# Splitting the first input projection's weights on VectorE, moving a block of constants, adding idle passes, and a new hand-written order

## The chip, the core and the metric

The kernel runs on one core of one Trainium2 chip. The core has a matrix engine (TensorE, written PE in the profile), three engines for elementwise work (VectorE, DVE; ScalarE, ACT; GpSimd, POOL), a queue that issues transfers (SyncE, SP) and 16 DMA engines behind it. Each engine works through its own instructions in order and waits for semaphores where it needs another's result. The metric is the device time of one execution in microseconds.

## The reference, cut to what matters

One layer over 256 latent tokens of 1024 channels, with 256 context tokens, batch 1, all in float32:

```python
mod_l = silu(c) @ w_ada + b_ada              # shifts, scales, gates
zl = modulate(rms_norm(x, norm1_g), sh1, sc1) @ w_in       # 1024 -> 2048 columns
zc = modulate(rms_norm(ctx, norm1_g), csh1, csc1) @ w_in   # same for the context
conv_l = silu(layer_norm(dwconv31(zl[:, :512] * sigmoid(zl[:, 512:1024]))))
lru_l = (forward_scan + backward_scan of gated coefficients) * gelu(zl[:, 1536:])
x = x + g1 * (concat(conv_l, lru_l) @ w_out)
h2 = modulate(rms_norm(x, norm2_g), sh2, sc2)
x = x + g2 * hier_moe(h2, ...)     # top group of 4, top 2 of its 8 experts
out = rms_norm(x, final_g)         # 32 experts, three 1024 x 1024 matrices each
```

The experts' weights are 32 x 3 x 4 MB = 402 MB; everything ahead of them reads some 40 MB.

## The kernel before

The kernel has two parts. The **prologue** computes everything up to the router's choice and the gather of the tokens of the first four experts. The **expert stage** streams all 32 experts' weights through nine tiles of 2 MB (`wide0` to `wide8`); expert by expert it multiplies, gates, turns, multiplies down and scatters back. In it the matrices w1 and w3 are read by `up` (line 874 issues the loads, line 877 multiplies).

*Memory.* The prologue's large buffers are 17 slots of 1 MB (`slot()`), handed out and taken back as the program goes; a float32 tile of 128 x 2048 fills one. When the prologue's pools are closed, the nine wide tiles take over the same memory, two slots to a tile, the ninth also over the `t512` buffers, among them those that the gather of line 815 reads. A wide tile is loaded as soon as everything that lay below has been used for the last time. `WORDER` is the order in which the nine are taken; all their loads are issued by SP, in that order, behind the prologue's own loads.

*First stage of the prologue.* Products that need more than one pass of precision are made from a high and a low half: `split_hi` copies a weight tile to a rounded format, `split_lo` subtracts that from the original (lines 298 to 303). The first projection (`vgproj`, line 331) goes in four quarters of 256 input channels. For quarter q: load the modulation weights and multiply (`ada_first`, line 244), copy the row out (`ada_rows`, ScalarE), turn it (`ada_turn`, TensorE), add bias and scale into columns (`ada_h`, VectorE, lines 268 and 273), modulate the activations (`modulated`: high half on ScalarE, line 292; rest and low half on VectorE, lines 293 and 294), split the quarter's weights (`load_wz`, `split_hi`, `split_lo`), and multiply for four column tiles. `ZH` and `ZL` name the engine of the high and the low half for each quarter (S ScalarE, V VectorE, G GpSimd). The weights of quarter q+1 are split ahead of its columns. The decay constants of the recurrent part (`kh`, `nkh`, lines 204 to 227) are computed on VectorE, with one exponential on ScalarE, ahead of the first quarter.

*Middle.* From the last quarter of `vgproj` on, all engines' work is issued in an order written out by hand, `ORDER`: each word is a step, the letter its kind, digits its arguments, `*n` a repetition. Each engine takes its own instructions from it in that order. The steps that matter here: `v` vgproj's last quarter for one column tile, `h`/`o` high and low half of the second projection's weights (ScalarE, GpSimd), `l` the gated unit that opens the convolution, `u` the second projection, `t` a convolution tap on VectorE, `s` one whose product is made on ScalarE and added on GpSimd, `i` the same with the product on VectorE (line 484), `b` a step of the later modulation, `I`/`J` high and low half of an output-projection weight (engines in `WH`, `WL`; only the third of four is split), `X` the same for its other operand, `O` a pass of the output projection (line 680), `M C Q R N` the layer norm, `n` the scans, `T` the router's top choices, `P` positions of tokens (line 750), `F` one-hot matrices (line 770), `Z` halves of the normed tokens (lines 781 and 303), `G` the gather's matmuls (line 815), `U` its results, `B` a small turn, `W` n idle passes (`warm(n)`, matmuls of ones into a bank that nobody reads, line 154).

## Time and profile before

| | us |
|---|---|
| median of the runs | 1118.24 |
| lowest, highest of 3 | 1113.62, 1120.35 |
| profiled execution, its time | 1117.2 |
| profiled execution, its span | 1115.4 |
| TensorE busy / weight loads | 1001.6 / 446.5 |
| VectorE, ScalarE, GpSimd busy | 311.7, 173.6, 104.0 |
| DMA, mean over the span | 399 GB/s |

All rows are of one profiled execution. A row of a timeline has start, duration, engine, line, operation, what is written and read, and in brackets the idle time ahead of it and what ended it. "PEclk" is the share of TensorE's full clock that was granted: 1.00 is 2.4 GHz, 0.50 is 1.2 GHz. Work of one engine that another hides costs nothing; what counts is what ended the wait of the next.

### The profile page before, as it was taken

The numbers are of one execution on the slowest core, as the hardware profiler recorded it, in microseconds if no ns is written. First come the engines' busy times: TensorE is split into PE (matmuls) and PEld (weight loads), VectorE is DVE, ScalarE is ACT, GpSimd is POOL, SyncE is SP. The second block draws the span as 40 slices with busy tenths as digits, with TensorE's granted clock in tenths as the row PEclk, the third lists the DMA queues.
The fourth block names the chain that finished last, engine by engine and source line by source line (L and its number), as shares of the span: only waits on it lengthen the run. The fifth ranks groups of instructions, "written<-read, shape, count | busy, mean of one in ns | idle before, by whom it ended". The sixth has DMA issues, their size and how long they took to land.

```text
span 1115.4 us, 11881 instructions
## 1 busy us (share of the span) xinstructions
PE 1001.6 (90%) x4973; PEld 446.5 (40%) x4973; DVE 311.7 (28%) x627; ACT 173.6 (16%) x329; POOL 104.0 (9%) x106
## 2 busy tenths in 40 slices
PE   7889998999999998988898898899898989898796
PEld 6764546343434342333333333233333333232244
DVE  4788975221121112111211121112121111111132
ACT  3457943200001000000000000000000000000002
POOL 2487443000000000000000000000000000000001
PEclk9899998999999999999999999999999999999998
DMA  9766759999999999999999999999999999999995
GB/s 360 273 228 266 300 201 420 386 431 431 431 430 430 430 431 431 432 430 429 430 430 432 431 432 430 430 429 431 429 432 431 430 430 431 431 432 431 430 415 198
DMA packets 48480, 445.21 MB, mean 399 GB/s; under 512 B 4084, under 2 KB 14372, under 8 KB 22053
## 3 DMA queue, kind: packets, MB, share of 16 engines
q1 hardware_dynamic: 48210, 443.84, 94.7%
q8 instruction: 41, 0.67, 0.2%
q10 hardware_dynamic: 210, 0.55, 0.1%
q14 instruction: 19, 0.15, 0.0%
HBM read 443.32 MB, written 1.05 MB: 398 GB/s over the span
## 4 chain that ended last, share of the span: by engine, by line
DMA 54%; PE 30%; DVE 1%; POOL 0%; issue 0%; ACT 0%; SPq 0%; DVEq 0%; POOLq 0%; ACTq 0%
DMA wide<-in_w_dram 54%; PE bank L877 20%; PE bank L789 3%; PE bank L680 2%; PE bank L898 2%; PE bank L815 1%; PE bank L1004 1%; PE bank L1134 0%; PE bank L511 0%; PE bank L537 0%; PE bank L1163 0%; PE bank L721 0%; PE bank L1043 0%; POOL xg L1179 0%; PE bank L891 0%
## 5 line engine op out<-in xcount | busy, mean ns | idle before, releaser
L877 PE MATMUL bank<-wide,xg 128*64 128x512 f32 x1984 | 449.0, 598 | 74.6 <-DMA wide<-in_w_dram 74.6
L877 PEld LDWEIGHTS bank<-wide,xg 128*64 128x64 f32 x1984 | 141.8, 137 | 366.1 <-issue 257.0
L877 PE MATMUL bank<-wide,gt 128*64 128x512 f32 x992 | 219.9, 595 | 1.3 <-DVE gt L1006 1.0
L987 DVE TENSOR_TENSOR sl<-sl,bank 128x512 f32<-128x512 f32 x31 | 21.3, 687 | 463.7 <-issue 440.1
L877 PEld LDWEIGHTS bank<-wide,gt 128*64 128x64 f32 x992 | 68.4, 137 | 140.4 <-issue 137.9
L1023 DVE TENSOR_TENSOR yy<-bank,g2bc 64x512 f32<-64x512 f32 x62 | 42.7, 689 | 191.9 <-PE bank L877 191.4
L1179 POOL TENSOR_TENSOR xg<-x,fgbc 128x256 f32<-128x256 f32 x6 | 4.7, 806 | 907.9 <-DVE x L1173 907.9
L980 ACT ACTIVATE sl<-bank 128x512 f32<-128x512 f32 x31 | 18.5, 597 | 431.0 <-PE bank L877 431.0
L789 PE MATMUL bank<-oh,xn 128*128 128x256 f32 x224 | 61.1, 416 | 0.0
L789 PEld LDWEIGHTS bank<-oh,xn 128*128 128x128 f32 x224 | 54.4, 327 | 11.4 <-issue 11.4
L898 PE MATMUL bank<-yy,st 128*128 128x512 f32 x120 | 58.0, 606 | 0.0
L1007 ACT COPY gt<-bank 128x256 f32<-128x256 f32 x31 | 11.5, 372 | 221.0 <-DVE gt L1006 221.0
L903 DVE TENSOR_TENSOR x<-x,bank 128x512 f32<-128x512 f32 x60 | 39.7, 683 | 7.1 <-PE bank L898 7.1
L795 ACT ACTIVATE xg<-bank,gsp 128x256 f32<-128x256 f32 x32 | 17.8, 563 | 153.5 <-PE bank L789 149.0
L303 POOL TENSOR_TENSOR slot<-slot 128x2048 fp32r<-128x2048 f32 x7 | 32.3, 4626 | 35.7 <-ACT slot L298 26.2
L331 PE MATMUL bank<-slot 128*128 128x256 f32 x192 | 28.4, 307 | 7.5 <-ACT slot L292 6.3
L898 PEld LDWEIGHTS bank<-yy,st 128*128 128x128 f32 x120 | 20.6, 191 | 26.5 <-issue 23.2
L798 DVE TENSOR_SCALAR xg<-bank,gsp 128x256 f32<-128x256 f32 x32 | 17.2, 543 | 47.2 <-ACT xg L795 47.1
L331 PEld LDWEIGHTS bank<-slot 128*128 128x128 f32 x192 | 26.2, 209 | 9.6 <-ACT slot L292 7.2
L377 PE MATMUL bank<-slot 128*128 128x512 f32 x96 | 22.9, 394 | 1.5 <-POOL slot L303 1.5
L1004 PEld LDWEIGHTS bank<-ident,sl 128*128 128x128 f32 x124 | 19.5, 204 | 11.1 <-issue 7.1
L487 POOL TENSOR_TENSOR xn<-xn,fgbc 128x256 f32<-128x256 f32 x30 | 22.5, 750 | 2.3
(255 smaller groups left out, 691.8 us busy)
## 6 DMA issues: line engine op xcount, KB each, us to landing
wide<-in_w_dram SPq DMA_DIRECT2D x186, 2048.0 KB, 38.7
slot<-in_wada_dram SPq DMA_DIRECT2D x16, 1024.0 KB, 7.0
slot<-in_wada_dram SPq DMA_DIRECT2D x16, 512.0 KB, 8.9
slot<-in_win_dram SPq DMA_DIRECT2D x8, 1024.0 KB, 7.9
wide<-in_w_dram SPq DMA_DIRECT2D x8, 1024.0 KB, 29.2
slot<-in_wout_dram SPq DMA_DIRECT2D x4, 1024.0 KB, 9.0
wide<-in_w_dram SPq DMA_DIRECT2D x8, 512.0 KB, 11.8
x<-in_x_dram SPq DMA_DIRECT2D x2, 512.0 KB, 4.2
```

The lines of the kernel that those rows point to most:

```text
L303: en.tensor_tensor(lo, w, f(hi), OP.subtract)
L331: P.matmul(pvg[ct][:, i * T:(i + 1) * T], wz[k // 2][wi][:, k % 2, c:c + 128], x[k // 4][:, k % 4, 0:T], start=k + i + n == 0, stop=k == 7 ...
L377: P.matmul(pu, w, x[k // 4][:, k % 4], start=k + n == 0, stop=k == 7 and n == 2)
L487: G.tensor_tensor(acc, acc, p, OP.add)
L680: P.matmul(p, m[:, q], w[:, c:c + 512], start=first and n == 0, stop=len(done) == 8 and n == len(passes) - 1)
L789: P.matmul(pg[:, i * 256:(i + 1) * 256], xn[:, t, quad(k)], oh[:, t].rearrange("p e s -> p (e s)"), start=t + i == 0, stop=t == 1 and i == ...
L877: P.matmul(ps[64 * h:64 * h + 64, :], xs(k4 * 4 + i), w[:, i, h * 512:(h + 1) * 512], start=k4 + i == 0, stop=k4 * 4 + i == 7, tile_positi ...
L898: P.matmul(pz, st[:, t * 128:(t + 1) * 128], yy[:, h * 512:(h + 1) * 512], start=True, stop=True)
L903: V.tensor_tensor(x1[:, t, q], x1[:, t, q], pz, OP.add)
L987: V.tensor_tensor(gg, sl, pb, OP.mult)
L1004: P.transpose(pt[:, j * 128:(j + 1) * 128], gg[:, quad(j)], ident)
L1023: V.tensor_tensor(yy[o:o + 64, h * 512:(h + 1) * 512], py[64 * h:64 * h + 64, :], g2bc[64 * h:64 * h + 64, h * 512:(h + 1) * 512], OP.mult)
```

## The change

- `ZL`: the low halves of the first projection's weights go from GpSimd to VectorE; in each quarter the columns and activations (`prepare`) now come ahead of the split of the quarter's weights, and a second computation of the first columns is gone.
- The decay constants move from ahead of the first quarter to the second pass of the loop, behind the split of quarter 2.
- `WH`: the high half of the split output-projection weight goes from VectorE to ScalarE. (`WL` changes only in a place that is not used.)
- `W4` and `W5`, four and five idle passes, stand ahead of `P0` and `F0`.
- `ORDER` is otherwise rearranged: nine `i` and 44 `s` in place of seven and 46, `l2` and one `b` earlier, scans `n31` and `n21` and several `O` and `G` in other places. `WORDER` is new.

```diff
--- before.py
+++ after.py
@@ -22,7 +22,7 @@
 SLOTS = 17
 WIDE = 9
 
-WORDER = (0, 7, 5, 2, 1, 6, 4, 3, 8)
+WORDER = (2, 7, 0, 6, 1, 3, 5, 4, 8)
 
 
 SP = 384
@@ -31,15 +31,15 @@
 
 
 ORDER = """
-v0 h0 o0 l0 v2 t v3 t h1 v1 t o1 u0 t*4 l2 u1 l1 t b t s b s t*2 s*2 t s t*2 s*2 t i t*2 s t l3 s*2 i t s t*4 s b t*2
-s t c1 t*2 s*3 t s*2 t*2 s*2 t s i t c0 b*2 s u2 s*2 t p10 c2 s t s t p11 t s p00 b s a10 t a00 t i*2 u3 w b t*2 p20 t
-i t*2 p01 s*2 c3 t p30 s*2 t*2 s t d10 s*2 i p21 t a20 s*2 t*2 d00 t a30 t d30 s t b t b z0 t s t a01 r1 d20 s q10 s*2
-t*2 b t*2 s L0 t*2 s q20 t*4 L4 z1 I0 s q30 t p31 q00 t n00 t*2 n20 s b d01 a11 M b a31 k1 C2 z2 C1 a21 n10 C0 L2 d11
-C3 d21 q11 b q21 q01 d31 z3 Q n01 b R e0 N1 N2 X1 N0 I2 L6 x b X2 N3 X0 n30 J2 J0 O001 e3 q31 O112 I4 e2 X3 n11 I6
-O012 O111 O010 J4 b e1 O002 O100 O011 O110 g O113 n31 O102 n21 m1 X5 j J6 m3 O101 O000 O003 X7 O103 m0 O005 O017 O007
-O013 r2 m2 X6 k2 X4 O006 O105 O104 O004 O015 O114 O014 D00 O107 O016 O115 D01 H00 O106 Y0 D10 O117 O116 H01 H10 y D11
-K00 H11 K01 K10 Z0 T0 K11 P0 F0 G06 B G04 G02 Y1 T1 G07 G05 P1 Z1 G03 G00 F1 A1 G01 G10 G11 G12 U0 G16 G17 G14 G15 U4
-U1 G13 U2 U3 U6 U5 U7 A0
+v0 h0 o0 l0 v2 t v3 t h1 v1 t l2 o1 u0 t*4 u1 l1 t b t s b t s t*2 s*2 t s t s*2 t i t*2 s b t s l3 s*2 t s t*4 s b
+t*2 s t c1 t*2 s*3 t s*2 t s*2 t s i t c0 b s u2 s*2 t p10 c2 s t s t p11 t s p00 b i a10 t a00 t i*2 t u3 w b t*2 p20
+t i t*2 p01 s*2 c3 t p30 s*2 t*2 s t d10 s*2 i p21 t a20 s*2 t*2 d00 t a30 t d30 i t b t b z0 t s t a01 r1 d20 i s q10
+s t*2 b t*2 s L0 t*2 q20 t s t*3 L4 z1 I0 s q30 t p31 q00 t n00 t*2 n20 s b d01 a11 M b a31 k1 C2 z2 C1 a21 n10 C0 L2
+d11 C3 d21 q11 b q21 q01 d31 z3 Q n01 b R e0 N1 X1 N2 N0 I2 L6 x b X2 N3 X0 n30 J2 J0 O001 e3 q31 O112 O102 n21 I4 e2
+X3 n11 n31 I6 O012 O111 O010 J4 b e1 O002 O100 O011 O110 g O113 m1 X5 j J6 m3 O101 O000 O003 X7 O103 m0 O017 O007 O013
+r2 m2 X6 k2 X4 O004 O005 O006 O105 O104 O015 O114 O014 D00 O107 O016 O115 D01 H00 O106 Y0 D10 O116 O117 H01 H10 y D11
+K00 H11 K01 K10 Z0 T0 K11 W4 P0 W5 F0 G06 B G04 G02 Y1 T1 G05 P1 Z1 G03 G00 F1 G07 A1 G01 G10 G11 G12 U0 G16 G17 U6
+G14 G15 U4 U1 G13 U2 U3 U5 U7 A0
 """
 VTAPS = (31, 0, 9, 31)
 
@@ -49,11 +49,11 @@
 SQ = ("SGGG", "SSSS")
 LNSQ = "SGSG"
 XC = ("VS", "SV")
-WH, WL = "SSVV", "VVGV"
+WH, WL = "SSSS", "GVGV"
 MH, ML = "GGGGGSSG", "GVGVGVGG"
 GL = ("GG", "GG")
 OS = "0010"
-ZH, ZL = "SSSS", "GGGG"
+ZH, ZL = "SSSS", "VVVV"
 FN = "VS"
 
 
@@ -201,32 +201,6 @@
     first_norm(1, xc)
 
 
-    kh = const.tile([128, 8], F32, name="kh")
-    nkh = const.tile([128, 8], F32, name="nkh")
-    lw = const.tile([128, 5, 8], F32, name="lw")
-    lam = col("lam")
-    V.tensor_scalar(lw[:, 0], lam, -1.0, None, OP.mult)
-    V.tensor_tensor(lw[:, 0], lam, lw[:, 0], OP.max)
-    S.activation(lw[:, 1], lw[:, 0], AF.Exp, scale=-1.0)
-    V.tensor_scalar(lw[:, 2], lw[:, 1], 2.0, None, OP.add)
-    V.reciprocal(lw[:, 2], lw[:, 2])
-    V.tensor_tensor(lw[:, 2], lw[:, 1], lw[:, 2], OP.mult)
-    V.tensor_tensor(lw[:, 3], lw[:, 2], lw[:, 2], OP.mult)
-    V.memset(lw[:, 4], 1.0 / 17.0)
-    for n in (15, 13, 11, 9, 7, 5, 3, 1):
-        V.tensor_tensor(lw[:, 4], lw[:, 4], lw[:, 3], OP.mult)
-        V.tensor_scalar(lw[:, 4], lw[:, 4], 1.0 / n, None, OP.add)
-    V.scalar_tensor_tensor(lw[:, 4], lw[:, 4], 2.0, lw[:, 2], OP.mult, OP.mult)
-    V.tensor_scalar(lw[:, 0], lam, -1.0, 0.0, OP.mult, OP.max)
-    V.tensor_tensor(kh, lw[:, 0], lw[:, 4], OP.add)
-    V.tensor_scalar(kh, kh, 4.0, None, OP.mult)
-    V.tensor_scalar(nkh, kh, -1.0, None, OP.mult)
-    hb = sp[:, COLS["ba"][0]:COLS["bx"][1]]
-    V.tensor_scalar(hb, hb, 0.5, None, OP.mult)
-    dwh = col("dw")
-    V.tensor_scalar(dwh, dwh, 0.5, None, OP.mult)
-
-
 
     mod_a = const.tile([128, 2, 2, 8], F32, name="mod_a")
     g1s = const.tile([128, 2, 8], F32, name="g1s")
@@ -318,7 +292,6 @@
 
     pa = ada_first(0)
     pt = ada_turn(ada_rows(pa))
-    ada_h(0, pt)
     warm(6)
     pvg = [bank() for _ in range(4)]
 
@@ -339,19 +312,45 @@
 
     engines = {"V": V, "S": S, "G": G}
     w = load_wz(0)
+    prepare(0)
     split_hi(*w, engines[ZH[0]])
     split_lo(*w, engines[ZL[0]])
-    prepare(0)
     for q in range(4):
         ks = range(2 * q, 2 * q + 2)
         if q < 3:
             w = load_wz(q + 1)
             rows = ada_rows(ada_first(q + 1))
-            split_hi(*w, engines[ZH[q + 1]])
-            split_lo(*w, engines[ZL[q + 1]])
             vgproj(0, ks)
             pt = ada_turn(rows)
             prepare(q + 1)
+            split_hi(*w, engines[ZH[q + 1]])
+            split_lo(*w, engines[ZL[q + 1]])
+            if q == 1:
+
+                kh = const.tile([128, 8], F32, name="kh")
+                nkh = const.tile([128, 8], F32, name="nkh")
+                lw = const.tile([128, 5, 8], F32, name="lw")
+                lam = col("lam")
+                V.tensor_scalar(lw[:, 0], lam, -1.0, None, OP.mult)
+                V.tensor_tensor(lw[:, 0], lam, lw[:, 0], OP.max)
+                S.activation(lw[:, 1], lw[:, 0], AF.Exp, scale=-1.0)
+                V.tensor_scalar(lw[:, 2], lw[:, 1], 2.0, None, OP.add)
+                V.reciprocal(lw[:, 2], lw[:, 2])
+                V.tensor_tensor(lw[:, 2], lw[:, 1], lw[:, 2], OP.mult)
+                V.tensor_tensor(lw[:, 3], lw[:, 2], lw[:, 2], OP.mult)
+                V.memset(lw[:, 4], 1.0 / 17.0)
+                for n in (15, 13, 11, 9, 7, 5, 3, 1):
+                    V.tensor_tensor(lw[:, 4], lw[:, 4], lw[:, 3], OP.mult)
+                    V.tensor_scalar(lw[:, 4], lw[:, 4], 1.0 / n, None, OP.add)
+                V.scalar_tensor_tensor(lw[:, 4], lw[:, 4], 2.0, lw[:, 2], OP.mult, OP.mult)
+                V.tensor_scalar(lw[:, 0], lam, -1.0, 0.0, OP.mult, OP.max)
+                V.tensor_tensor(kh, lw[:, 0], lw[:, 4], OP.add)
+                V.tensor_scalar(kh, kh, 4.0, None, OP.mult)
+                V.tensor_scalar(nkh, kh, -1.0, None, OP.mult)
+                hb = sp[:, COLS["ba"][0]:COLS["bx"][1]]
+                V.tensor_scalar(hb, hb, 0.5, None, OP.mult)
+                dwh = col("dw")
+                V.tensor_scalar(dwh, dwh, 0.5, None, OP.mult)
             for ct in range(1, 4):
                 vgproj(ct, ks)
     wu = []
```

## Rows read from the trace of the kernel before

**Rows 1.** Windows: stretch, length, busy (x) of PE PEld DVE ACT POOL, PEclk, DMA share, GB/s

```profile
71.00:103.00 32.00, 31.77 (x174) 19.50 (x178) 25.73 (x45) 21.09 (x40) 26.69 (x36) 1.00 0.51 187
...
103.00:138.00 35.00, 31.68 (x175) 15.87 (x168) 32.64 (x58) 32.12 (x55) 17.65 (x22) 1.00 0.88 342
...
29.10:39.30 10.20, 7.28 (x34) 6.70 (x35) 8.05 (x23) 4.03 (x6) 4.29 (x1) 0.54 0.64 237
...
186.00:196.40 10.40, 8.84 (x66) 8.53 (x66) 6.08 (x29) 5.05 (x10) 3.02 (x3) 0.55 1.01 431
...
196.00:200.00 4.00, 4.00 (x19) 2.35 (x21) 1.72 (x6) 1.67 (x4) 0.00 (x0) 1.00 0.49 150
...
200.00:400.00 200.00, 196.80 (x877) 77.23 (x875) 37.70 (x79) 17.14 (x36) 0.00 (x0) 1.00 1.01 430
...
400.00:600.00 200.00, 178.91 (x778) 67.98 (x776) 35.73 (x69) 11.22 (x24) 0.00 (x0) 1.00 1.01 431
```

**Rows 2.** Timeline of SP: the first and the fourth load of wide tiles.

```profile
155.13 1.10 SPq L874 DMA_DIRECT2D wide<-in_w_dram  x2
...
167.40 0.33 SPq L874 DMA_DIRECT2D wide<-in_w_dram  x1
```

**Rows 3.** Waits of SP: who waited for whom, us in total, times, longest.

```profile
SPq L874 <- PE bank L815: 19.0, 1, 19.0
...
SPq L874 <- PE bank L680: 5.2, 1, 5.2
```

**Rows 4.** Timeline of the first stage, quarters 0 to 2.

```profile
20.74 0.17 DVE L211 TENSOR_SCALAR lw<-lw 128x8 f32<-128x8 f32 x1 [5.79 <-ACT lw L210]
...
22.25 0.33 PE L263 MATMUL bank<-ident,t 128*128 128x128 f32 x1 [0.39 <-ACT t L258]
...
22.41 1.50 PE L154 MATMUL bank<-ones 128*128 128x128 f32 x12
...
24.07 4.53 POOL L303 TENSOR_TENSOR slot<-slot 128x2048 fp32r<-128x2048 f32 x1 [9.92 <-ACT slot L298]
...
24.25 4.38 DVE L218 TENSOR_SCALAR lw<-lw 128x8 f32<-128x8 f32 x1
...
30.91 2.08 ACT L292 ACTIVATE slot<-slot,mod_a,g1s 128x256 fp32r<-128x256 f32 x4 [6.92 <-DVE g1s L273]
...
31.56 0.79 PE L331 MATMUL bank<-slot 128*128 128x256 f32 x2 [4.58 <-ACT slot L292]
...
44.75 4.55 PE L331 MATMUL bank<-slot 128*128 128x256 f32 x36
```

**Rows 5.** Timeline, quarter 3 and the start of the middle.

```profile
53.63 4.46 DVE L273 SCALAR_TENSOR_TENSOR g1s<-mod_a,sp 128x2 f32<-128x2 f32 x2
...
62.20 0.39 ACT L441 ACTIVATE t<-bank 128x256 f32<-128x256 f32 x1 [0.28 <-PE bank L331]
...
71.23 8.00 PE L377 MATMUL bank<-slot 128*128 128x512 f32 x34 [1.54 <-POOL slot L303]
```

**Rows 6.** Lines by form: count, duration min/median/max (or busy us, mean ns).

```profile
L294 DVE TENSOR_TENSOR slot<-slot x16: 424/426/428, 32.0 to 61.5; 128x256 fp32r<-128x256 f32 x16
...
L987 DVE TENSOR_TENSOR sl<-sl,bank 128x512 f32<-128x512 f32 x31 | 21.3, 687 | 463.7 <-issue 440.1
...
L298 ACT CAST slot<-slot x6: 1885/1903/1906, 22.1 to 62.5; 128x2048 fp32r<-128x2048 f32 x6
...
L484 DVE TENSOR_SCALAR fgbc<-cb,sp x3: 342/348/348, 97.8 to 109.1; 128x256 f32<-128x256 f32 x3
```

**Rows 7.** Timeline of the routing and the gather.

```profile
186.72 0.61 PE L750 MATMUL bank<-msk,tri 128*128 128x32 f32 x2 [2.75 <-DVE msk L745]
...
188.17 0.81 PE L815 MATMUL bank<-oh,t 128*128 128x256 f32 x2 [0.83 <-DVE oh L770]
...
191.73 2.70 POOL L303 TENSOR_TENSOR t<-xn,t 128x512 fp32r<-128x512 f32 x2 [5.41 <-ACT t L781]
...
192.25 5.39 PE L815 MATMUL bank<-oh,t 128*128 128x256 f32 x22
```

## What is expected of the change

> **What bounds the kernel now.** I read the kernel from its end backwards, with the windows by stretch first. From 200 to 400 and from 400 to 600 us the DMA engines' share is 1.01 at 430 and 431 GB/s, while TensorE gets down to 178.91 busy of 200 us [rows 1]: the expert stage ends when its weights have landed. So I asked when that stream starts to run without a hole. Nine expert loads go into the nine wide tiles before any tile is reused; the first is issued at 155.13 us [rows 2]. The ninth waited 19.0 us for the matmuls of line 815 [rows 3], the gather for the first four experts, because its tile lies over buffers that the gather reads. The last of these matmuls ends at 192.25 + 5.39 = 197.64 [rows 7]. The eight loads ahead of it were through just before: from 196 to 200 the DMA share is 0.49 [rows 1], a hole worth 4 x 0.51 = 2.0 us, the only one from there on. **A microsecond off the end of the gather is therefore a microsecond off the kernel**, as long as eight loads are in by then; a stream that only starts earlier gives nothing, since it waits longer for the ninth tile.
>
> The gather's end hangs on the work in front of it. In 71 to 103 us TensorE is busy 31.77 of 32 us, in 103 to 138 VectorE 32.64 of 35 and ScalarE 32.12 [rows 1]; a shift at 71 us travels through, less what is added on VectorE behind 103. The stage ahead of 62 us (quarter after quarter: modulation columns, activations, weight halves, products) is where the change works. There the columns are late: the turned modulation is ready at 22.25 + 0.33 = 22.58, yet the activations begin at 30.91 [rows 4]. A VectorE instruction on 8 columns takes 4.38 us, from 24.25, exactly under GpSimd's 4.53 us subtraction of the low half; the rest of the constants, and then the columns, stand behind it in VectorE's queue. In the last quarter two column instructions take 4.46 us in the same way [rows 5].
>
> **The change, part by part.**
>
> *Low halves on VectorE (ZL), and columns ahead of them.* The operation is not in the trace on VectorE at 128x2048. By its rows at 256 and 512 elements (0.426 and 0.687 us, 1.02 ns per element) it is 0.687 + 1536 x 0.00102 = 2.25 us [rows 6]; bounds are 2.1 (the slope alone) and 4.6 (GpSimd's own time). I take 2.25. Quarter 0: columns from 22.6 to about 23.1 (one of two computations of them is removed), activations on ScalarE 2.08 us to 25.2, high half 1.90 to 27.1, low half to 29.4. TensorE's products of column tile 0 then wait for 29.4, and their last four (0.126 us each, 4.55 / 36) end at 29.9; before, the first began at 31.56 [rows 4]. Turn at 30.3, columns 30.7, activations and high half (2.08 + 1.90) at 34.8, low half at 37.1. TensorE: 36 products to 34.8, about 2 us of modulation matmuls to 36.8 (their weights have landed: this queue is unchanged up to there), the next quarter's first products to 38.3, turn at 38.6. Quarter 2 likewise: columns 39.1, high half 43.1, low half 45.4; turn of quarter 3 at 46.9.
>
> *Constants later.* They now stand on VectorE between that low half (45.4) and the columns of quarter 3. They are 30 instructions at a pitch of about 0.2 us (from 20.74 to 24.25 eighteen of them begin [rows 4]), plus the hop to ScalarE for one exponential: 6.4 us, so columns 3 start at 51.8 and not at 46.9. At their old place they held the first columns; what waits behind them now are activations, both halves and products of quarter 3. Bounds: 5 us if they follow each other without a gap, and 8 if the hops show. Columns done 52.25, activations 54.35, high half 56.25, low half 58.5. Before, the columns of quarter 3 ended at 53.63 + 4.46 = 58.1 [rows 5], but both halves were ready by then. So of 6 us of lead, about half goes back.
>
> *TensorE in front of the last quarter.* Its products (now ORDER's v0) start at 56.25 after idling from 51.45, 4.8 us. The trace has this case: idle 4.58 us ahead of 31.56 [rows 4], and a granted clock of 0.54 from 29.1 to 39.3 [rows 1], the 1.2 GHz level for nearly all of it. I take half of such a stretch: v0 ends at about 59.6, the tanh that opens the convolution follows there (before: 62.20 [rows 5]), and all 48 products end at 65.2. The second projection's low halves stay on GpSimd; they end at 58.5 + 2 x 4.53 = 67.6; before, TensorE's wait for them ended at 71.23 [rows 5]. With 48 matmuls of 0.235 us (8.00 / 34) from 65.2 on, TensorE is through at 76.5 in place of 71.23 + 8.00 = 79.2. **Shift at this point: -2.7 us**; -3.5 with no fall of the clock, +0.6 if all 48 products run at the low one.
>
> *The middle.* ORDER has nine of the side taps' products on VectorE in place of seven: 2 x 0.35 = +0.7 us [rows 6], in the part where VectorE is the fullest; ScalarE loses as many. Bounds: 0 (ScalarE was as full) and 2, if each also waits for a GpSimd add to end. WH moves the high half of one output-projection weight to ScalarE, 1.90 us [rows 6] in a queue with idle time around 150, and its low half on GpSimd starts some 3 us later. Behind it wait GpSimd's products for the recurrent columns and so the last output-projection passes; ORDER puts these passes later by about as much. I cost it at nothing; without that cover up to 3 us. The removed column computation is worth 0.4 us and is contained above.
>
> *Idle passes.* W4 stands in a hole: TensorE idles 2.75 us ahead of 186.72 [rows 7]. W4's eight rows and W5's ten take 1.0 and 1.25 us at the rate of 12 in 1.50 [rows 4]. W5 fills a wait of 0.83 us and so costs 0.4. From 186.0 to 196.4 the granted clock is 0.55 [rows 1], and 22 gather matmuls take 5.39 us. At full clock 32 of them need 32 x 0.126 = 4.0 us in place of some 8. But the second token tile's low halves leave GpSimd only at 191.73 + 2.70 = 194.43 [rows 7], and five of its eight blocks need or stand behind the later one: ten matmuls, 1.3 us, end at 195.7. **Gain 1.9 us**, not 4. If the clock falls all the same, W5 costs 10 x 0.25 = 2.5 us in the hole of 0.83: **+1.7**. The Trainium skill (TensorE: Matmul & The Clock Gate, Part 1) holds that the throttled state is the default and that sustained activity releases it. By it these passes, at 2.4 GHz, keep the gain; the trace shows the low level through 10.4 us with TensorE busy 8.84 of them, which is why I do not count on it, and by that row the sum would be 3.6 us higher.
>
> *WORDER.* It picks which wide tile is loaded first. A first load before 155.13 [rows 2] is worth nothing by itself, by the argument above; one up to 2.0 us later is free too, since it closes the hole ahead of the ninth.
>
> *Sum*: -2.7 + 0.7 - 1.9 = -3.9. The profiled execution took 1117.2 us (span 1115.4 and 1.8 around it): 1113.3. It lies 1.0 below the median of 1118.24, so the median forecast is **1114.3 us**. All best ends: -3.5 + 0 - 1.9, and near 2 more if the constants take 5 us: 1111. All worst ends of the same mechanism, 0.6 + 1.9 + 1.7: 1122.
>
> **Rivals.**
> *The clock falls anyway ahead of the gather* (the passes don't do what they are for). For: the row of 10.4 us at 0.55. Against: W4 and W5 are full 128-column passes where there was nothing. -2.0 + 1.7 = -0.3: 1118.
> *The lead is lost in the middle*: three engines over 90% busy in 103 to 138, so ORDER's lead dissolves and only the gather's gain stays: 1116.3. For: ScalarE and VectorE are both full. Against: all three are full of the same work as before, started earlier.
> *More than forecast*: the constants' hops are short and the clock holds at 56: about -8: 1110.
> *Slower: the first expert load waits for the output projection.* WORDER begins with tile 2. In the old layout tile 2 was the fourth, and its load waited for output-projection matmuls of line 680 until 167.40 [rows 2, 3]. All wide loads are in one queue behind it. If the new layout has it alike, the first issue is at 167.4 - 2.0 = 165.4, 10.3 us later than before, of which the hole takes 2.0: +8.3, 1126. It decides once the first issue is later than 157.1. Against: the slots are handed out in another order after the change, so tile 2 need not hold the same weights; the trace cannot say.
>
> **How the numbers follow.** Forecast 0.45 (its own range 1111 to 1117), clock falls 0.22, lead lost 0.13, more 0.12, slower rival 0.08. The range 1107 to 1121 leaves out the slower rival and the far end of the better one. One per cent is 11 us, about what a measurement of this kernel can tell from no change; only several best ends together reach it, or a much later first load: faster 0.06, same 0.90, slower 0.04.
>
> **What would show it.** VectorE's low halves near 2.25 us with no VectorE instruction on few columns over 1 us before 56; columns 0 by 23; the constants between 45 and 52 with columns 3 behind them; the tanh near 59.6; line 815's end near 193.7; clock 1.0 from 184 on; the first wide issue before 157.1 and the DMA with a hole only ahead of the ninth. Wrong would be: the ninth load not waiting for the gather, a DMA hole after 200, or TensorE idle inside the output projection.

## The result, and the profile after the change

The median fell from 1118.13 us to 1111.84 us (20 runs of each): ratio 0.995, interval 0.9941 to 0.9959. The gain is half a per cent and clear of none; it is within the 1% that the forecast called "same", 2.5 us below the predicted 1114.3 and inside its range. The profiled execution took 1111.8 us, its span 1110.0 against 1115.4. Line numbers have moved: gather 814 (815 before), wide loads 873 (874), low halves 277 (303), columns 242 (268), first products 304 (331).

The first stage, in order of time (columns as in [rows 4]; the second fence is TensorE alone):

```profile
22.77 0.17 DVE L242 TENSOR_TENSOR mod_a<-bank,sp 128x8 f32<-128x8 f32 x1 [7.85 <-PE bank L237]
...
27.07 2.29 DVE L277 TENSOR_TENSOR slot<-slot 128x2048 fp32r<-128x2048 f32 x1
...
38.24 0.17 DVE L242 TENSOR_TENSOR mod_a<-bank,sp 128x8 f32<-128x8 f32 x1 [1.34 <-PE bank L237]
...
44.76 0.17 DVE L334 TENSOR_SCALAR lw<-sp 128x8 f32<-128x8 f32 x1
...
50.51 0.17 DVE L242 TENSOR_TENSOR mod_a<-bank,sp 128x8 f32<-128x8 f32 x1
...
56.64 9.46 POOL L277 TENSOR_TENSOR slot<-slot 128x2048 fp32r<-128x2048 f32 x2 [42.24 <-ACT slot L272]
...
58.40 0.39 ACT L440 ACTIVATE t<-bank 128x256 f32<-128x256 f32 x1 [1.83 <-PE bank L304]
```

```profile
54.82 1.51 PE L304 MATMUL bank<-slot 128*128 128x256 f32 x8 [4.33 <-ACT slot L272]
...
64.32 11.07 PE L376 MATMUL bank<-slot 128*128 128x512 f32 x48
...
140.09 0.71 PE L166 MATMUL bank<-ident,r 128*128 128x128 f32 x4 [0.41 <-POOL r L160]
...
142.35 5.42 PE L679 MATMUL bank<-slot,xn 128*128 128x512 f32 x12
```

In this stage no VectorE instruction on few columns is long any more where [rows 4, 5] had 4.4 us ones. The low half takes 2.29 us. The constants run from 44.76 to 50.5 with columns 3 behind them, and TensorE idles 4.33 us ahead of the last quarter. The second projection ends at 64.32 + 11.07 = 75.39.

The gather, then the DMA engines around its end (windows: stretch, length, busy of PE PEld DVE ACT POOL, PEclk, DMA share, GB/s), then SP's first wide load and its longest wait for the gather:

```profile
186.10 6.05 PE L814 MATMUL bank<-oh,t 128*128 128x256 f32 x24
...
186.44 2.69 POOL L277 TENSOR_TENSOR t<-xn,t 128x512 fp32r<-128x512 f32 x2 [5.73 <-ACT t L780]
186.53 1.47 DVE L769 TENSOR_TENSOR oh<-iota,posm 128x256 fp32r<-128x256 f32 x1
```

```profile
189.00:190.00 1.00, 1.00 (x6) 1.00 (x6) 0.90 (x5) 0.57 (x1) 0.14 (x1) 1.00 0.86 352
190.00:191.00 1.00, 1.00 (x6) 1.00 (x6) 0.67 (x3) 0.22 (x1) 0.00 (x0) 1.00 0.16 66
191.00:192.00 1.00, 1.00 (x5) 0.95 (x5) 0.00 (x0) 0.62 (x2) 0.00 (x0) 1.00 0.04 16
192.00:193.00 1.00, 1.00 (x7) 0.35 (x7) 0.21 (x1) 0.76 (x2) 0.00 (x0) 1.00 0.00 0
...
196.00:400.00 204.00, 200.80 (x897) 78.67 (x895) 38.08 (x76) 16.77 (x33) 0.00 (x0) 1.00 1.01 431
```

```profile
144.73 0.33 SPq L873 DMA_DIRECT2D wide<-in_w_dram  x1
```

```profile
SPq L873 <- PE bank L814: 19.1, 1, 19.1
```

The first wide load now goes out at 144.73, ten us earlier than in [rows 2], and yet the ninth again waits 19.1 us for the gather. What the early start shows in the DMA engines is a longer hole: 0.14 + 0.84 + 0.96 + 1.00 = 2.9 us without traffic, against 2.0 before [rows 1]. From 196 us on the stream is full (share 1.01, 431 GB/s).

The end of the gather moved from 197.64 [rows 7] to 192.15, by 5.49 us; the span by 5.4. In two pieces: line 166, the norm ahead of the output projection, moved from 144.17 to 140.09, and the way from it to the gather's end shrank from 53.47 to 52.06 us. The kernel before at that place (timeline, then a window):

```profile
144.17 1.20 PE L166 MATMUL bank<-ident,r 128*128 128x128 f32 x4 [0.41 <-POOL r L160]
...
147.98 4.56 PE L680 MATMUL bank<-slot,xn 128*128 128x512 f32 x10
```

```profile
144.00:150.00 6.00, 5.83 (x35) 3.14 (x36) 5.70 (x10) 4.04 (x8) 0.11 (x1) 0.72 0.01 3
```

The table gathers these points for all traces. They are single executions that come out of their start unevenly (column "turn 0", the first turned modulation, at 20.8 to 24.6 us; const_early's 26.5 is its own doing), so lengths are compared rather than points. "Projection" is the end of the second projection's first 48 matmuls. The ratio stands against runs of the kernel before on the same chip; medians of different rows are of different chips, and rows are better compared by their ratios.

| kernel | turn 0 | columns 3 | projection | line 166 | gather's end | span less gather's end | median | ratio, interval |
|---|---|---|---|---|---|---|---|---|
| before | 22.25 | 53.43 | 79.23 | 144.17 | 197.64 | 917.8 | 1118.13 | |
| after | 22.40 | 50.51 | 75.39 | 140.09 | 192.15 | 917.9 | 1111.84 | 0.995, 0.9941 to 0.9959 |
| stage_alone | 24.56 | 52.66 | 77.56 | 142.49 | 194.44 | 924.7 | 1118.00 | 0.9999, 0.9983 to 1.0014 |
| old_worder | 22.40 | 50.50 | 74.41 | 139.12 | 191.78 | 923.7 | 1118.12 | 1.0015, 1.0004 to 1.0025 |
| no_idle | 22.56 | 50.67 | 75.79 | 140.50 | 192.62 | 918.0 | 1113.42 | 0.9953, 0.9938 to 0.9967 |
| contiguous | 22.56 | 50.65 | 74.41 | 139.14 | 192.02 | 917.8 | 1113.70 | 0.9976, 0.9963 to 0.9988 |
| contiguous_write | 20.75 | 49.32 | 73.08 | 137.78 | 190.68 | 917.7 | 1110.91 | 0.9944, 0.9924 to 0.9963 |
| lows_on_vectore | 22.65 | 50.75 | 74.53 | 139.26 | 191.87 | 917.9 | 1111.38 | 0.9941, 0.9918 to 0.9964 |
| low_on_gpsimd | 22.45 | 56.81 | 83.80 | 148.52 | 202.82 | 917.8 | 1120.47 | 1.0034, 1.002 to 1.0047 |
| const_first | 22.38 | 51.15 | 74.86 | 139.57 | 192.35 | 917.8 | 1111.45 | 0.9941, 0.9919 to 0.9962 |
| const_last | 24.59 | 48.36 | 74.53 | 148.16 | 199.93 | 917.8 | 1117.62 | 0.9998, 0.9983 to 1.0013 |
| const_early | 26.53 | 51.33 | 75.09 | 139.80 | 191.63 | 917.9 | 1111.10 | 0.9947, 0.9935 to 0.9959 |
| const_gap | 22.42 | 46.62 | 70.34 | 135.05 | 187.83 | 917.8 | 1106.47 | 0.9902, 0.988 to 0.9925 |
| gap_and_gather | 20.96 | 45.78 | 69.50 | 134.22 | 185.16 | 918.6 | 1106.78 | 0.99, 0.9883 to 0.9916 |

In eleven of fourteen traces the span ends 917.7 to 918.0 us after the gather: its end sets the kernel's. Two that are far off, stage_alone and old_worder, have the old WORDER behind the new first stage in common; of the third, gap_and_gather, below.

Two stretches take longer in some traces than in others, with the same code, where the granted clock is low. Seven traces have the changed first stage (after to lows_on_vectore); from turn 0 to the projection column they take 51.9 to 53.2 us, after 52.99, the kernel before 56.98. In after the clock is 0.50 from 56 to 62 us, while TensorE multiplies; in old_worder, with 52.01, it is 0.50 from 54 to 60, partly while TensorE waits. And the 24 matmuls of line 720 in front of the routing take 2.77 us at the full clock and some 4 at the low one, in seven traces: old_worder, contiguous, contiguous_write, lows_on_vectore, low_on_gpsimd, const_first and const_gap. There the way from line 166 to the gather's end is some 0.8 us longer (52.67 to 52.78 in old_worder, const_first and const_gap, whose gather is the changed kernel's, against 51.8 to 52.1).

### The profile page after: what moved, and what is told of

It reads as the page before. It is cut to its first block, busy times and chain, and to the rows that moved or that the text cites. A ratio compares the mean times of both kernels' runs of the same rounds, so it can differ in the third digit from the quotient of the medians.

```text
span 1110.0 us, 11919 instructions
## 1 busy us (share of the span) xinstructions
PE 1002.1 (90%) x4991; PEld 447.7 (40%) x4991; DVE 303.6 (27%) x629; ACT 175.2 (16%) x328; POOL 84.5 (8%) x102
## 4 chain that ended last, share of the span: by engine, by line
DMA 55%; PE 36%; DVE 4%; POOL 1%; ACT 1%; issue 1%; SPq 0%; POOLq 0%; DVEq 0%; ACTq 0%
DMA wide<-in_w_dram 55%; PE bank L876 20%; PE bank L788 3%; PE bank L679 2%; PE bank L376 2%; PE bank L897 2%; PE bank L304 1%; DVE bank L468 1%; PE bank L510 1%; PE bank L814 1%; PE bank L1003 1%; DVE slot L277 1%; ACT slot L272 0%; PE bank L186 0%; PE bank L396 0%
## 5 line engine op out<-in xcount | busy, mean ns | idle before, releaser
L897 PEld LDWEIGHTS bank<-yy,st 128*128 128x128 f32 x120 | 20.6, 191 | 26.5 <-issue 23.2
L679 PE MATMUL bank<-slot,xn 128*128 128x512 f32 x48 | 22.2, 601 | 0.0
```

The source lines that it names most:

```text
L679: P.matmul(p, m[:, q], w[:, c:c + 512], start=first and n == 0, stop=len(done) == 8 and n == len(passes) - 1)
L897: P.matmul(pz, st[:, t * 128:(t + 1) * 128], yy[:, h * 512:(h + 1) * 512], start=True, stop=True)
```

## Experiments: which part brought the time

**stage_alone.** The first stage as changed, everything behind it as before:

```diff
-WORDER = (2, 7, 0, 6, 1, 3, 5, 4, 8)
+WORDER = (0, 7, 5, 2, 1, 6, 4, 3, 8)
...
-v0 h0 o0 l0 v2 t v3 t h1 v1 t l2 o1 u0 t*4 u1 l1 t b t s b t s t*2 s*2 t s t s*2 t i t*2 s b t s l3 s*2 t s t*4 s b
+v0 h0 o0 l0 v2 t v3 t h1 v1 t o1 u0 t*4 l2 u1 l1 t b t s b s t*2 s*2 t s t*2 s*2 t i t*2 s t l3 s*2 i t s t*4 s b t*2
...
-WH, WL = "SSSS", "GVGV"
+WH, WL = "SSVV", "VVGV"
```

> The changed kernel's first stage (low halves on VectorE, columns ahead of them, constants in the second pass) with ORDER, WORDER and WH of the kernel before, so without idle passes. If the gain was made in the first stage alone: the row of the norm (line 166) starts at 139.4 to 140.1 us as in the changed kernel (140.09; before 144.17), and the kernel takes 1111 to 1112 us unless the clock falls behind it as it did before, which costs 1.5 us. If the new order is what carries the lead through the middle: that row starts at 142 us or later and the kernel takes 1114 to 1118 us.

By its numbers this is the second theory's outcome (line 166 at 142.49, 1118.00 us), but not by its mechanism: line 166 is late only because turn 0 is, at 24.56. From turn 0 to line 166 it takes 117.93 us, the changed kernel 117.69, the one before 121.92; from there to the gather's end 51.95, the changed one 52.06. So the lead of four us is the first stage's. What the new ORDER and WH are worth up to line 166 shows from the projection column on: 64.93 and 64.94 us in stage_alone and before, 64.70 to 64.73 in all traces with the new ORDER but const_last. They save 0.2 us. And yet nothing arrives at the end: 924.7 us from the gather's end on. Waits of SP, then windows:

```profile
SPq L873 <- PE bank L679: 33.7, 3, 21.1
...
SPq L873 <- PE bank L814: 18.5, 1, 18.5
```

```profile
170.00:175.00 5.00, 5.00 (x18) 2.63 (x17) 3.37 (x5) 0.72 (x2) 1.14 (x3) 1.00 0.53 157
190.00:195.00 5.00, 5.00 (x24) 4.58 (x25) 1.97 (x10) 2.51 (x8) 1.25 (x1) 0.92 1.00 424
```

The loads wait for the output projection (line 679), the DMA engines are busy for half of 170 to 175, and at 190 to 195, where the changed kernel has its hole, they are busy throughout: the ninth load waits for the gather as before and goes out behind it, but queues behind others.

**old_worder.** The changed kernel with one line of before:

```diff
-WORDER = (2, 7, 0, 6, 1, 3, 5, 4, 8)
+WORDER = (0, 7, 5, 2, 1, 6, 4, 3, 8)
```

> The changed kernel with the old order of the wide tiles, (0, 7, 5, 2, 1, 6, 4, 3, 8); all else stays. Forecast (an earlier start of the stream is worth nothing, the ninth load waits for the gather): the gather's end stays, the kernel stays at 1111 to 1112.5 us. Theory from the run with the first stage alone (its third load was issued at 172.13 us, behind the output projection, and its gather's end came as early as in the changed kernel, but the kernel was 7 us longer): the third load waits until about 169.7 us, the six behind it need some 29 us, the DMA runs without a hole past the gather's end, and the kernel takes 1117 to 1119.5 us.

The theory taken from stage_alone holds, the forecast's does not: 1118.12 us. The first two loads go out at 155.81 and 156.26, the third at 168.47 behind the output projection. A tile of 128 x 4096 floats is 2.10 MB, by estimate 4.88 us at 430 GB/s; six of them from 168.5 on last to 197.8, past the gather's end at 191.78. SP's issues, from the third load on, then windows:

```profile
168.47 4.05 SPq L873 DMA_DIRECT2D wide<-in_w_dram  x6
```

```profile
165.00:170.00 5.00, 5.00 (x20) 3.15 (x19) 1.96 (x3) 0.58 (x3) 0.00 (x0) 1.00 0.65 226
...
190.00:195.00 5.00, 5.00 (x24) 2.79 (x25) 2.27 (x9) 2.18 (x6) 0.00 (x0) 1.00 1.01 433
```

Without the new WORDER the whole gain is lost (ratio 1.0015 against 0.995). That the new first stage hands out the slots in another order, so that the old tile order no longer fits the times at which tiles come free, is an argument from the program; no run shows which slots lie under which tile, and the new WORDER was not run in the old layout.

**low_on_gpsimd.** The first stage's main edit undone, the rest kept:

```diff
-ZH, ZL = "SSSS", "VVVV"
+ZH, ZL = "SSSS", "GGGG"
```

> The changed kernel with ZL back at GpSimd; columns stay ahead of the weights' halves, all else stays. Forecast's reading (GpSimd needs 4.53 us where VectorE needs 2.29, and VectorE's few-column instructions crawl under it): each of the three quarter steps is 2.2 us longer, the constants take about 10 us because they start under the subtraction of quarter 2, columns 3 come at about 57 in place of 50.5, the second projection's low halves end near 75 in place of 66.1, and the kernel takes 1118 to 1121 us. Rival (the order of columns ahead of the halves is what brought the gain, the engine little): 1112 to 1115 us.

As expected, to the place: columns 3 at 56.81, the second projection's low halves end at 61.15 + 13.63 = 74.78, 1120.47 us. With the columns ahead of the halves, but the low halves on GpSimd, the kernel is slower than the one before. Part of that is the constants, which take 10.1 us here in place of 5.75: in the first row a VectorE instruction on 8 columns lasts exactly as long as GpSimd's subtraction.

```profile
46.88 4.56 DVE L335 TENSOR_TENSOR lw<-sp,lw 128x8 f32<-128x8 f32 x1
...
56.81 0.17 DVE L242 TENSOR_TENSOR mod_a<-bank,sp 128x8 f32<-128x8 f32 x1
```

```profile
46.86 4.56 POOL L277 TENSOR_TENSOR slot<-slot 128x2048 fp32r<-128x2048 f32 x1 [5.30 <-ACT slot L272]
```

## Experiments: the idle passes and the gather

**no_idle.** `W4` and `W5` are taken out of ORDER.

```diff
-K00 H11 K01 K10 Z0 T0 K11 W4 P0 W5 F0 G06 B G04 G02 Y1 T1 G05 P1 Z1 G03 G00 F1 G07 A1 G01 G10 G11 G12 U0 G16 G17 U6
+K00 H11 K01 K10 Z0 T0 K11 P0 F0 G06 B G04 G02 Y1 T1 G05 P1 Z1 G03 G00 F1 G07 A1 G01 G10 G11 G12 U0 G16 G17 U6
```

> The changed kernel without its idle passes W4 and W5; all else stays. Theory of the forecast (the passes keep the clock up, and the clock sets the pace of the gather): the granted clock falls in front of the gather, its last matmul ends about 1.9 us later than 192.15, the kernel takes 1113.7 us against 1111.8. Rival (the gather's matmuls do not follow the clock: 22 in 5.39 us at 0.50 before, 24 in 6.05 us at 1.00 after, 0.245 and 0.252 us each): the clock may fall, but the gather's end moves by -0.4 to +0.3 us and the kernel stays at 1111.4 to 1112.1.

The way from line 166 to the gather's end is 52.12 us without and 52.06 with them. The median, 1113.42, lies near the first theory's 1113.7, but its ratio can't be told from the changed kernel's (0.9953 against 0.995, overlapping intervals), so the traces decide. The clock does what the forecast feared (the gather's last matmuls stand under the windows):

```profile
180.00:185.00 5.00, 2.65 (x39) 2.33 (x40) 3.69 (x21) 0.57 (x2) 0.95 (x4) 0.50 1.03 439
185.00:190.00 5.00, 5.00 (x23) 5.00 (x23) 2.67 (x10) 4.05 (x9) 2.56 (x2) 0.50 1.02 431
```

```profile
186.59 6.02 PE L814 MATMUL bank<-oh,t 128*128 128x256 f32 x24
```

Through these ten us it is 0.50, the 1.2 GHz level; in the changed kernel 0.68 and 0.98: there too it is 0.50 from 182 to 185, in spite of the passes. The gather's last 24 matmuls take 6.02 us here, all at 0.50, and 6.05 there, at 1.00. They do not follow the clock. (The rival's 22 in 5.39 us "at 0.50" were not all at that level: the clock over them is 0.71.) The trace of the kernel before shows it within one stretch of these matmuls:

```profile
193.00:195.00 2.00, 2.00 (x11) 2.00 (x10) 1.12 (x7) 1.15 (x4) 1.43 (x2) 0.50 0.97 418
...
196.00:197.00 1.00, 1.00 (x5) 1.00 (x6) 0.15 (x1) 0.00 (x0) 0.00 (x0) 1.00 0.48 205
```

Eleven in 2 us at 0.50, five in 1 us at 1.00.

**contiguous.** What else sets their pace? A block's 128 weights are picked with a step of four elements, 16 bytes. Here the halves are stored so that they lie side by side:

```diff
-            S.mul(w[1], x1[:, t, q], rstd[:, t:t + 1])
-            split_lo(*w, engines[GL[t][h]])
+            xq, wh, wl = (xn[:, t, q].rearrange("p (c k) -> p k c", k=4),
+                          *(v.rearrange("p (k c) -> p k c", k=4) for v in w[1:]))
+            S.mul(wh, x1[:, t, q].rearrange("p (c k) -> p k c", k=4), rstd[:, t:t + 1])
+            split_lo(xq, wh, wl, engines[GL[t][h]])
...
-            P.matmul(pg[:, i * 256:(i + 1) * 256], xg_s[t, k // 4][n][:, quad(k % 4)],
+            P.matmul(pg[:, i * 256:(i + 1) * 256], xg_s[t, k // 4][n][:, k % 4 * 128:k % 4 * 128 + 128],
```

> The changed kernel with the two halves of the normed tokens for the first gather stored so that a block's 128 channels lie side by side; ScalarE and GpSimd read their inputs with a stride of four elements, TensorE's weights are contiguous. If the stride of the weights sets the pace of the gather (0.24 us a matmul at either clock; the same shape with contiguous weights takes 0.126 us at line 304): line 814's pitch falls to 0.12 to 0.14 us at the full clock, the last low half still leaves GpSimd at about 189.1, the gather ends near 190.9 in place of 192.15, the kernel takes 1110 to 1111 us. Rival (the pace is set by something else, such as the moving side): pitch 0.23 or more, kernel unchanged.

Timeline of TensorE, of ScalarE and of GpSimd, then the weight loads of the changed kernel and of this one (count, duration min/median/max in ns):

```profile
186.67 1.36 PE L816 MATMUL bank<-oh,t 128*128 128x256 f32 x9
189.25 0.96 PE L816 MATMUL bank<-oh,t 128*128 128x256 f32 x6 [1.22 <-POOL t L277]
190.72 1.30 PE L816 MATMUL bank<-oh,t 128*128 128x256 f32 x9 [0.51 <-POOL t L277]
```

```profile
186.40 2.31 ACT L782 ACTIVATE t<-x,rstd 128x512 fp32r<-128x512 f32 x2
```

```profile
187.67 3.00 POOL L277 TENSOR_TENSOR t<-xn,t 128x512 fp32r<-128x512 f32 x2 [6.90 <-ACT t L782]
```

```profile
L814 PEld LDWEIGHTS bank<-oh,t x32: 308/332/336, 182.8 to 191.6; 128*128 128x128 f32 x32
```

```profile
L816 PEld LDWEIGHTS bank<-oh,t x32: 186/188/338, 183.6 to 191.6; 128*128 128x128 f32 x32
```

24 matmuls now take 1.36 + 0.96 + 1.30 = 3.62 us of TensorE in place of 6.05, and a weight load 188 ns in place of 332: the step of the weights sets the pace. (At the low clock, up to 186 us, this kernel's loads take about 330 ns as well and start every 0.22 us, with the step every 0.24: it costs little there.) The gather's end does not come earlier (52.88 us from line 166, where traces with the same low clock in front of the routing have 52.67 to 52.78): ScalarE's two halves take 2.31 in place of 1.33 us, GpSimd's 3.00 in place of 2.69, and TensorE waits 1.22 and 0.51 us for them. The Trainium skill (Advanced Engine Details and Errata, SBUF Cachelines) says that SBUF works in lines of 16 bytes and that each access that goes to another line pays; four floats are such a line, and the trace agrees for TensorE's weights (6.05 against 3.62 us) and for ScalarE's reads (2.31 against 1.33).

**contiguous_write.** The same, but read in order and written with a step, here of 128 elements, 512 bytes (`"p (k c) -> p c k"` on the written side).

> As the run with contiguous gather weights, but with the elements taken in their stored order and written with a stride: ScalarE and GpSimd read in order and write four channels 512 bytes apart. If reading with a stride was what made ScalarE's half 1.15 us in place of 0.66, and writing with one costs nothing: ScalarE 0.66, GpSimd's last low half at 189.1, gather at a pitch of 0.126 us and its end near 190.8, kernel 1110 to 1111 us. Rival (a stride costs the same on either side): ScalarE 1.15 us, gather's end at 192, kernel as the changed one.

ScalarE's halves take 2.15 us, GpSimd's 3.02, the way to the gather's end 52.90: this step on the written side costs about as much. (The runs of contiguous spread from 1110.1 to 1116.5, and its ratio, 0.9976, is worse than this kernel's, 0.9944, and the changed one's; the traces do not explain it.)

**lows_on_vectore.** The other cover by itself: low halves of the second token tile on VectorE.

```diff
-GL = ("GG", "GG")
+GL = ("GG", "VV")
...
-K00 H11 K01 K10 Z0 T0 K11 W4 P0 W5 F0 G06 B G04 G02 Y1 T1 G05 P1 Z1 G03 G00 F1 G07 A1 G01 G10 G11 G12 U0 G16 G17 U6
+K00 H11 K01 K10 Z0 T0 K11 W4 P0 W5 F0 G06 B G04 G02 Y1 T1 G05 P1 F1 Z1 G03 G00 G07 A1 G01 G10 G11 G12 U0 G16 G17 U6
```

> The changed kernel with the second token tile's low halves for the gather on VectorE in place of GpSimd, and F1 ahead of Z1 in ORDER. If GpSimd's lock is what makes the one-hot matrix take 1.47 us (186.53; 0.43 for the first token tile): it takes 0.43, the low halves are done near 188.4 in place of 189.1, and the gather, then held by TensorE's pitch of 0.235 us alone, ends near 191.7 in place of 192.15: kernel 0.3 to 0.5 us shorter, not to be told from none. Rival (VectorE's low halves push the routing behind them, and the gather's results come later): gather's end at 192.5 or later.

The one-hot matrix takes 0.43 us in place of 1.47, the low halves are done at 187.57 + 0.69 = 188.3. The gather's end is 52.61 us behind line 166, at most 0.2 nearer than in traces with the same low clock in front of the routing (52.67 to 52.78): with this cover gone it is held by TensorE's pace.

```profile
186.38 0.43 DVE L769 TENSOR_TENSOR oh<-iota,posm 128x256 fp32r<-128x256 f32 x1
...
187.57 0.69 DVE L277 TENSOR_TENSOR t<-xn,t 128x512 fp32r<-128x512 f32 x1 [0.17 <-PE bank L814]
```

## Experiments: the place of the constants

**const_first.** The block of constants goes back ahead of the first quarter (the reverse of its move in the diff of the change).

> The changed kernel with the decay constants back ahead of the first quarter. Forecast's reading (the constants hold up whatever columns stand behind them, by some 4 to 5 us wherever they are): they run from 20.7 to 26.6, columns 0 come at about 26.8 in place of 22.8, and as the quarters follow one another every 7.7 us, columns 3 come at about 50.0 (now 50.5): the kernel takes 1111 to 1112 us. Rival (only GpSimd's subtraction made them slow at that place): columns 0 by 24, columns 3 by 47.2, kernel near 1108.5.

They end at 26.0 and columns 0 come at 25.98, columns 3 at 51.15: 0.6 us later than in the changed kernel, not 0.5 earlier, since the products of quarter 0 ran at a low clock behind TensorE's wait (36 in 5.71 us in place of 4.56, the clock 0.80 in 34 to 40 us). The last quarter keeps the full clock in return. Line 166 and the median are those of the changed kernel. Moving the block was worth nothing by itself.

**const_last.** The same block behind the loop over the quarters.

> The changed kernel with the decay constants behind the last quarter's low half on VectorE. If they cost what the forecast says at their new place (columns 3 wait for them from 45.9 to 50.5), and a lead at 60 us travels through: columns 3 at 45.9, TensorE's last quarter at about 50.2 with no fall of the clock, the kernel 3 to 4.6 us shorter, 1107.2 to 1108.8. Rival: the taps of the convolution now start behind them on VectorE, the fullest engine of the middle, or the second projection's weights come no sooner, and the lead dissolves: 1111 to 1113 us.

Wrong in its price. The rival had the place, VectorE in front of the taps, but not what makes it dear. Columns 3 do come without a wait and TensorE starts the second projection earlier, but (VectorE, then GpSimd):

```profile
57.41 4.57 DVE L344 TENSOR_SCALAR lw<-lw 128x8 f32<-128x8 f32 x1
62.01 4.48 DVE L343 TENSOR_TENSOR lw<-lw 128x8 f32<-128x8 f32 x1
...
69.35 0.42 DVE L439 SCALAR_TENSOR_TENSOR g2bc<-t,bank 128x256 f32<-128x256 f32 x1
```

```profile
57.37 9.10 POOL L277 TENSOR_TENSOR slot<-slot 128x2048 fp32r<-128x2048 f32 x2 [40.83 <-DVE lw L343]
```

The block meets the second projection's low halves on GpSimd, and two of its instructions take 4.57 and 4.48 us. The convolution opens at 69.35 (its input was ready at 57.57), line 166 comes 123.57 us behind turn 0 (117.69 in the changed kernel), and the gain is gone.

**const_early.** The block in VectorE's idle 7.85 us ahead of the first columns:

```diff
+    V.tensor_scalar(lw[:, 0], lam, -1.0, None, OP.mult)
+    V.tensor_tensor(lw[:, 0], lam, lw[:, 0], OP.max)
+    S.activation(lw[:, 1], lw[:, 0], AF.Exp, scale=-1.0)
     first_norm(1, xc)
+    V.tensor_scalar(lw[:, 2], lw[:, 1], 2.0, None, OP.add)
...
```

> The changed kernel with the decay constants where VectorE idled 7.85 us ahead of the first columns (14.9 to 22.8): their first two instructions and the exponential ahead of the context's norm, the rest behind it. If a lead at the last quarter travels through (in the run with the constants first, 0.5 us at columns 3 gave 0.5 us at line 166): columns 0 stay at 22.8, columns 3 come at 45.9 in place of 50.5, no VectorE instruction on few columns over 1 us, TensorE idles under 1 us ahead of the last quarter, the row of line 166 comes 3 to 4.6 us earlier, the kernel takes 1107.2 to 1109 us. Rival (the middle is bound by VectorE and takes the lead back): under 1 us of gain, 1111 to 1112 us.

Columns 0 come at 26.90, four us late. ScalarE's queue tells why:

```profile
15.22 0.21 ACT L207 ACTIVATE lw<-lw 128x8 f32<-128x8 f32 x1 [8.11 <-DVE lw L206]
15.33 1.04 ACT L178 ACTIVATE xn<-slot 128x1024 f32<-128x1024 f32 x1
```

The exponential waited 8.11 us for VectorE, and the context's squares, which start at 8.31 in the changed kernel, stood behind it. Lost in front, won at columns 3: line 166 at 139.80.

**const_gap.** The same with the three instructions issued between the context's diagonals and its copies:

```diff
-    def first_norm(s, src):
+    def first_norm(s, src, between=lambda: None):
...
             V.tensor_scalar(diag[:, 2 * s + t], ident, rstd_t[:, t:t + 1], None, OP.mult)
+        between()
```

> The changed kernel with the decay constants in VectorE's idle stretch ahead of the first columns, mended: in the run before, the exponential stood in ScalarE's queue ahead of the context's squares and waited there for VectorE, so the squares came at 15.2 us in place of 8.0 and columns 0 four us late (26.9). Now the first two constants and the exponential stand behind the diagonals of the context's norm (14.4 us), ahead of its copies. Expected: columns 0 at 22.8, columns 3 near 46, line 166's row 4 to 4.6 us earlier than in the changed kernel (140.09), kernel 1107 to 1108.5 us. Rival (the middle takes the lead back): kernel 1110.5 to 1112 us.

```profile
14.86 0.17 DVE L208 TENSOR_SCALAR lw<-sp 128x8 f32<-128x8 f32 x1
...
20.45 0.22 DVE L229 TENSOR_SCALAR sp<-sp 128x124 f32<-128x124 f32 x1
22.78 0.17 DVE L270 TENSOR_TENSOR mod_a<-bank,sp 128x8 f32<-128x8 f32 x1 [2.11 <-PE bank L265]
...
46.62 0.17 DVE L270 TENSOR_TENSOR mod_a<-bank,sp 128x8 f32<-128x8 f32 x1 [1.73 <-PE bank L265]
```

Now the block is free: columns 0 at 22.78, columns 3 at 46.62, line 166 at 135.05, 5.0 us earlier than in the changed kernel, and 1106.47 us (ratio 0.9902, its interval clear of the changed kernel's). Of the 5.0 us, 3.9 are there at columns 3; 1.2 more come by the projection column, as TensorE's wait of 4.33 us ahead of the last quarter is gone and the clock stays at 1.00 in 50 to 60 us. So the constants did hold up columns 3 in the changed kernel, and a lead at 50 us travels through to the end.

**gap_and_gather.** const_gap with contiguous_write and lows_on_vectore, as each of the last two had ended on the other's limit.

> The constants in VectorE's idle stretch (as in the run before), the gather's weights contiguous (written with a stride), and the second token tile's low halves on VectorE behind its one-hot matrix. Each of the last two alone gave nothing at the end: with contiguous weights the gather waited for GpSimd's low halves (1.19 and 0.54 us), with the low halves on VectorE it was held by TensorE's pitch of 0.235 us. If these two hide each other: low halves of 0.69 us on VectorE, done about 1 us earlier than GpSimd's, gather at 0.126 us a matmul without a wait over 0.5 us, its end some 2 to 2.7 us closer to line 166's row than 52.8 us, kernel 1103.5 to 1105 us. Rival (VectorE slows down with the stride as ScalarE did, or the eight loads are not in by then): kernel 1106 to 1107 us.

```profile
182.83 2.32 PE L817 MATMUL bank<-oh,t 128*128 128x256 f32 x15 [0.56 <-DVE t L305]
```

```profile
181.73 2.04 DVE L305 TENSOR_TENSOR t<-xn,t 128x512 fp32r<-128x512 f32 x2
```

The gather's end is 50.94 us behind line 166, 1.1 us better than the changed kernel's 52.06; VectorE pays for the step as well (2.04 us for two in place of 1.38). 0.8 us are given back behind the gather (918.6 in the table). The expert's inputs leave VectorE 2.67 us behind the gather's end there and 2.09 in const_gap; that this is the reason was not tested. By the ratio, 0.99 against 0.9902, it can't be told from const_gap.

## Why the prediction was right, and which of its steps were not

The time was right, in part by luck: the sum behind it had one term too small, two that did not come true and one missing, and these errors partly cancel.

*The bound.* "A microsecond off the end of the gather is therefore a microsecond off the kernel": shown. The condition behind it, "as long as eight loads are in by then", decides as well, but the forecast measured it at the wrong place. It says that a first load up to 2.0 us later is free and that the slower rival decides once the first issue is later than 157.1. In old_worder the first issue is at 155.81 and the kernel loses the whole gain, by the third load. The rival's mechanism was real; it threatened the old tile order in the new layout, not the new one. The sum has no term for WORDER, since an earlier first load is worth nothing by itself; but WORDER is what lets the gain through.

*First stage, forecast -2.7 at the end of the second projection.* Measured 75.39 against 79.23 [rows 5]: -3.8, or -4.0 from turn 0 on (3.8 to 5.1 in the seven traces with this stage). The mechanism is as told (low half 2.29 us against 2.25; columns of quarter 2 at 38.24 against 39.1; constants in front of columns 3; a wait of 4.33 us against 4.8 ahead of the last quarter, with a granted clock of 0.78 in 50 to 60 us). The mis-sized terms: the constants took 5.75 us in place of 6.4, and quarter 2's low half ended at 44.84 in place of 45.4, so that columns 3 came at 50.51 and not 51.8 and the tanh at 58.40 and not 59.6.

*Middle, forecast +0.7.* Measured -0.2: from the end of the second projection's 48 matmuls to line 166 it takes 64.70 us in place of 64.94, and stage_alone, with the old ORDER, takes 64.93. What the two more `i` cost by themselves was not run.

*Idle passes, forecast -1.9.* Failed, by its price: "at full clock 32 of them need 32 x 0.126 = 4.0 us". The 0.126 was taken from line 331 [rows 4], a matmul of the same shape with weights that lie side by side. The gather's weights have a step of 16 bytes; at 0.50 and at 1.00 of the clock they take 0.25 us each, so there was nothing to gain from the clock. The trace of the kernel before has both levels within these matmuls, at one pace. For the same reason the rival "the clock falls anyway" could cost little: in no_idle it fell for ten us at next to no cost. It also came true in part: in the changed kernel the clock is 0.50 from 182 to 185 us, and the forecast's sign, 1.0 from 184 on, came at 186.

*What was not in the sum.* The way from line 166 to the gather's end became 1.41 us shorter. The stretch up to the first output-projection pass gives 1.55: it took 3.81 us before (144.17 to 147.98, granted clock 0.72 in 144 to 150) and 2.26 after at 1.00, with the clock at 1.00 ahead of it in both. The rest of the way is 0.1 longer. Whether the clock falls there differs from trace to trace: of the fourteen it fell in before and in low_on_gpsimd, and stage_alone, with the old ORDER, kept it. What decides it was not settled, so 1.5 of the 5.5 us can't be put down to an edit.

So -3.9 stood for -4.1 (stage and middle) and +0.1 (the rest of the way, idle passes included), with -1.5 from a clock that held. Without the 1.9 us that the idle passes did not bring, the forecast would have been 1116.2. The rival "more than forecast", 1110, is nearer to the measured 1111.84 than the forecast. It named the right direction, constants shorter than told, but put the rest on the clock ahead of the last quarter, which did fall.

## What to carry to other kernels

When tiles are loaded into memory that other work frees, count all the loads ahead of the gating one, not the first: after a change upstream an order of loads that fitted may have to be fitted again. Before a faster clock is credited to a stretch of matmuls, look for the same line at both clock levels, and take the price from the same layout of weights; here the trace of the kernel before already had both levels. A block of tiny instructions is free only in a hole that no GpSimd operation covers; then also ask what stands behind its one foreign instruction in the other engine's queue.

## What the runs showed of the hardware

- Matmuls of 128x128 by 128x256 with weights at a step of 16 bytes: 0.25 us each at either clock level (24 in 6.02 us at 0.50 in no_idle and 24 in 6.05 at 1.00 in the changed kernel). Side by side, in contiguous: 9 in 1.36 us. The load of the weights takes 332 ns with the step and 188 side by side (medians); at the low clock it takes about 330 side by side too.
- For two instructions on 128x512 floats, ScalarE takes 2.31 us with a step of 16 bytes on the read side and 2.15 with one of 512 bytes on the written side, in place of 1.33; VectorE's subtraction 2.04 with the 512-byte step, in place of 1.38; GpSimd's 3.00 and 3.02, in place of 2.69.
- One GpSimd subtraction of 128x2048 held a VectorE instruction on 8 columns for its whole length (4.56 us under 4.56 in low_on_gpsimd), and a block of them met it once per GpSimd instruction, not once in all (4.57 and 4.48 under two in const_last).
